# Mixture-of-experts kernel: a taken-branch prefetch hint for each expert's overflow branch on three engines

## The chip, the cores and the metric

The kernel runs on one core of a Trainium2 chip. The metric is the device time of one execution in microseconds (us), the median of several runs. A core has five engines with an instruction stream of their own each: TensorE (PE in the rows; PEld is its weight load), VectorE (DVE), ScalarE (ACT), GpSimd (POOL) and SyncE (SP, which here issues most DMAs). Each engine has a sequencer that reads the stream, waits on semaphores, takes branches and hands work to the engine; a row with a q behind the engine's name (PEldq, DVEq) is the sequencer's.

## The reference

Two transformer blocks on 256 tokens of width 1024. The change lies in the last part, a mixture of experts:

```python
def hierarchical_moe(h, w_group, b_group, w_expert, b_expert, w_gate, w_up, w_down):
    ...
    gates = ...   # top 1 group of 4, then top 2 of its 4 experts, per token
    y = jnp.zeros_like(t)
    for e in range(N_EXPERTS):                     # 16
        a = jax.nn.silu(t @ w_gate[e]) * (t @ w_up[e])
        y = y + gates[:, e:e + 1] * (a @ w_down[e])
    return y.reshape(h.shape)
```

Each expert has 1024 x 512 gate and up weights and 512 x 1024 down weights in float32, 6.3 MB in all. A token goes to two of the 16 experts.

## The kernel before, in words

The kernel does not compute every expert for every token. It numbers the tokens of each expert, gathers the first 64 of them with one-hot products, runs the expert on these 64 slots, and adds the weighted result back with another one-hot product. Tokens beyond the first 64 are handled in up to four further passes of 32, 64, 64 and 32 slots (`MORE`, line 152), which are nested under conditions.

The function `experts` (line 1839) is one unrolled loop over the 16 experts, traced in order. For expert e:

- `ahead` and `take` (lines 1811 and 1831) issue the loads of weight tiles on SP, as far ahead as 20 tiles of 1 MB go; an expert takes six of them.
- `gated` (line 1902) finishes the expert before: VectorE multiplies its down product by the gates (L1912), ScalarE and VectorE split the result into two parts (L1916, L1917).
- `hidden` (line 1863) is the gate and up product: 32 matmuls of 128x512 into the bank `gu`, then the SiLU on ScalarE (L1872) and the product on VectorE (L1873).
- Products for other experts fill TensorE's wait for these two: for even e the combination of the pair before (`combine`, bank `cmb`), for odd e the one-hot transposes (`places`, bank `ohT`), and half of the gather for the next pair (`gather`, bank `ga`).
- `down` (line 1876) transposes the hidden values (bank `aT`, L1887) and does 16 matmuls into the bank `dn`.
- `others` (line 1942) tests the expert's bit in a word that all engines hold in a register, and under it lies the code of the overflow passes, `more` (line 1920):

```python
with tc.If((words[i] & (1 << e)) > 0):        # L1946
    more(e, w, p, S)
    if i + 1 < len(MORE):
        others(e, w, i + 1)
```

Each engine has this branch in its own stream. An engine that has no overflow to do jumps over the body and adds to two semaphores what the body would have added (the EVENT_SEMAPHORE rows of L1946). With this data only expert 0 has overflow, of one pass of 32 slots. Work after the branch on other engines, and the reuse of the expert's weight tiles, waits for these semaphores. Order on an engine is that of the trace, with `issue_after(x)` placing what is traced inside it behind instruction x.

All matmuls are issued in `mm` at L223, so the rows tell them apart by the banks' names.

Of the kernel before, what the change touches and what calls it, by code (L numbers as in the profile page):

```python
# [12 lines left out]
AF = mybir.ActivationFunctionType  # L13
# [5 lines left out]
P = 128  # L19
# [122 lines left out]
def tile_model(ctx: ExitStack, tc: tile.TileContext, aps: dict, out: bass.AP, dbg=None):  # L142
# [38 lines left out]
    def banks(**tags):  # L181
        """a new sharing of the banks: A for the main stream, F for those beside it, others for what names them"""
        pst.close()
        psum["pool"] = pst.enter_context(tc.tile_pool(name="ps" + "".join(tags), bufs=1, space=PSUM))
        psum["tags"] = tags
# [7 lines left out]
    # work beside the main stream, traced in steps between its tiles of weights  # L193
# [3 lines left out]
    def pool(name):  # L197
        """a pool of the stream that is traced: the second one has its own end of the memory"""
        return tc.tile_pool(name=name, bufs=1, side="right" if tagsel[0] == "F" else "left")
# [51 lines left out]
    def wsplit(raw, a, n):  # L251
        """split [P, a, n] in pieces of 1024 columns; returns k -> (hi, lo) of [P, n]"""
# [18 lines left out]
    # ---------------------------------------------------------------- modulation  # L271
# [35 lines left out]
    def gemv(m, s):  # L307
        """2048 columns of the modulation: row 32 * g of the result holds columns 512 * g.. (row 32 * g + 1 for the
        context's condition)"""
# [45 lines left out]
    def mods(m, parts):  # L355
        """the modulation of layer m (of the second block for m = 2)"""
# [16 lines left out]
    # ---------------------------------------------------------------- norms  # L373
# [16 lines left out]
    def rstd_x():  # L390
        """1 / rms of the rows of X, from the sums of squares of their halves"""
        rs = sp.tile([P, 2], F32, tag="rs2", name="rs2", bufs=2)
        nc.gpsimd.tensor_add(rs, SSQ[:, :, 0], SSQ[:, :, 1])  # L393
        rsq(rs, rs, 1.0 / D, EPS)
        return rs

    def norm_steps(a, sh, hi, lo, src=None, xsplit=None):
        """hi/lo [P, KT, 256] get the split of norm(x) * a + sh, transposed"""
# [46 lines left out]
    def out_proj(w, lh, ll, gd, first=None, after=None):  # L445
        """X += g * (lhs^T @ w); lh, ll [P, KT, 256]; first(n): the tile of the first four blocks of rows; after(n):
        what comes once half n of the columns is done"""
# [23 lines left out]
    # ---------------------------------------------------------------- layer 0 mixer  # L471
    def hybrid(begin, gates):
        w = aps["hy_w_in"]
        with ExitStack() as stack:
# [47 lines left out]
            # xBC^T and dt^T, weights stationary: [channel, lat 256 | ctx 256]  # L522
# [38 lines left out]
            # rope tables with the gains of the norms  # L561
# [10 lines left out]
            def rope(x, nh, i, b, dst):  # L572
                """dst = rope(x * gain); x [P, nh, 64]"""
# [9 lines left out]
            # k, v for latents and context  # L583
# [36 lines left out]
            # q  # L620
# [28 lines left out]
            # z^T  # L649
# [34 lines left out]
            # attention: the scores of a head lie in the queue ahead of the transposes of the head before  # L684
# [41 lines left out]
            # group norm of y * silu(z), [channel, tok]  # L726
# [24 lines left out]
            def first(n):  # L751
                # these rows of w_out follow the (kv, d) partition order of the attention output
# [10 lines left out]
    def ssd(hp, xbc, dtT, gy):  # L763
        # dt, decays: [tok, blk(lat0, lat1, ctx0, ctx1), dir*8 + head]
# [13 lines left out]
        # inclusive sums over the chunk, and the sums beyond each token (over both chunks for the context)  # L778
# [20 lines left out]
        # token-major copies of x and b  # L799
# [21 lines left out]
        # chunk states [ (g, n), head-in-group, p ]  # L821
# [23 lines left out]
        # per pair of heads (j, j + 4): decays from rows of inclusive sums, then both directions in one product  # L845
# [49 lines left out]
    def softplus(o, x, pool, name):  # L895
        """o = max(x, 0) + ln(1 + exp(-|x|))"""
# [6 lines left out]
    # ---------------------------------------------------------------- swiglu  # L903
# [65 lines left out]
    # ---------------------------------------------------------------- layer 1 mixer  # L969
# [37 lines left out]
    def final(i):  # L1007
        """x = norm(x) * w"""
# [11 lines left out]
    # ---------------------------------------------------------------- second block  # L1020
    def proj_tok(w, c0, hi, lo):
        """[tok, 512] per block of tokens: (h @ w[:, c0:c0 + 512])"""
# [10 lines left out]
    def proj_T(w, c0, hi, lo):  # L1033
        """(h @ w[:, c0:c0 + 512])^T of 256 tokens: two banks of [channel, 2 tiles, tok]"""
# [12 lines left out]
    def log_forget(f, lf, kf):  # L1047
        """lf = log sigmoid(f), kf = 1 - sigmoid(f); the floor of the forget gate is softmax over the one
        layer less itself, zero for any hg_lb"""
# [10 lines left out]
    def hg_ctx(hi, lo, S):  # L1060
        """final states [d, dir, head, e] of the context"""
        w = aps["w_in_2"]
        with pool("hgc") as hp:
# [4 lines left out]
            for dr in range(2):  # L1068
# [6 lines left out]
                for b in range(2):  # L1075
                    o = bank()
                    # sums beyond each token in the direction of the scan
# [25 lines left out]
    def hg_raw(hi, lo, raw, i):  # L1103
        """the logits of forget gate i (as U), or q for i = 2, all [channel, head, tok]"""
# [9 lines left out]
    def hg_gates(raw, hp, bufs):  # L1114
        """log decays A = log sigmoid(f) and U = -log(1 - sigmoid(f)) (in the place of f) of both directions"""
# [15 lines left out]
    def hg_rest(hi, lo, raw, i):  # L1131
        """values (i = 0) or weighted output gate, [tok, (head, e)]"""
# [9 lines left out]
    def hg_core(A, U, q, v, g, S, mh, ml, res):  # L1142
        """attention between tokens whose indices in the chunk first differ in bit lv, with decays split at the
        boundary between them; lv 7 is that between the chunks. Queries grow by A, keys decay by U: the input gate
        and the decay up to the boundary"""
        with tc.tile_pool(name="hgl", bufs=1) as hp:
# [4 lines left out]
            # the scores across the chunks take the place of U, which is done with by then  # L1151
# [64 lines left out]
    def head_norm(o, g, pre, sq, mh, ml, k0, c):  # L1216
        """rms norm over each head (of o * pre), times g (the weighted gate); the split transposed into mh/ml"""
# [18 lines left out]
    def dn_conv(i, hi, lo, lat, res, dp, hp, bufs):  # L1236
        """projects q, k or v (i = 0, 1, 2); returns the steps that convolve it, to [channel, head, tok]"""
# [39 lines left out]
    def dn_gates(hi, lo, res, dp, hp):  # L1277
        """gate and decay logits, [b_fwd, b_bwd, a_fwd, a_bwd] x head"""
# [11 lines left out]
    def dn_core(res, S, lat, dp, both):  # L1290
        """delta rule over two chunks of 128; S [d, dir, head, e] is left by the context and read by the latents;
        the split of the latents' output goes to the pair res["done"]"""
# [4 lines left out]
        with pool("dn") as hp:  # L1297
# [36 lines left out]
            # per chunk and direction, [s, head, t]: decays between tokens as sums of what lies between them, then  # L1334
            # the inverse of the unit triangular system by doubling its diagonal blocks: with y the inverse of the
            # blocks, y a y joins their early tokens (rows) with their late ones (columns)
# [49 lines left out]
            def half(t, m, i):  # L1386
                """columns of [P, 4, 128] in the first (i = 0) or second halves of blocks of 2 m"""
                return t.rearrange("p h (n s m) -> p h n s m", s=2, m=m)[:, :, :, i, :]
# [78 lines left out]
            if lat:  # L1467
                # 1 / |q| per token; q itself stays as it is, its norm goes on the output
# [96 lines left out]
    def mixer2(Shg, Sdn, a, sh):  # L1565
        w = aps["w_in_2"]
        with tc.tile_pool(name="m2", bufs=1) as mp, ExitStack() as right:
# [6 lines left out]
            with tc.tile_pool(name="hgr", bufs=1) as rp:  # L1574
# [28 lines left out]
                # the projections are done with the input: the mixer's output takes its place  # L1603
# [12 lines left out]
    # ---------------------------------------------------------------- mixture of experts  # L1616
    def router(a, sh):
        """the router's weights and bias with the modulation in them; returns the steps that follow the halves of
        X: its transposition and the logits [tok, block, group and expert]"""
# [32 lines left out]
    def route(lg, rp):  # L1652
        """lg [P, 2, 20]: membership [P, 2, 16] of the top 2 experts in the top group, and the gates as later()"""
# [8 lines left out]
        def first_max(v, n, name):  # L1662
            """per group of 4: the maximum and the one-hot of its first place"""
# [49 lines left out]
    def moe(a, sh, lg, rsx):  # L1713
        """gates and places of the tokens, then the experts: each takes its first 64 tokens, and under branches of
        its own the others"""
        with tc.tile_pool(name="moe", bufs=1) as mp:
# [4 lines left out]
            def onehot(q):  # L1721
                """[tok, block, expert of the pair, slot], and the same times 1 / rms(x)"""
# [12 lines left out]
            def gather(ohr, xg, ks):  # L1735
                """the tokens' x, modulated, [d, slot], for blocks ks of d; the last two as the returned steps"""
# [24 lines left out]
            # the sums over the experts start from x  # L1761
# [7 lines left out]
            with tc.tile_pool(name="rt", bufs=1) as rp:  # L1769
                sel, later = route(lg, rp)  # L1770
                # number of each token among its expert's tokens, from 1; 0 for those of other experts
# [13 lines left out]
                # bit e of word i: expert e has tokens for pass i of MORE  # L1785
# [9 lines left out]
    def wloader(wp):  # L1795
        """loads the experts' weights in the order of their use, as far ahead as the buffers go: those of wp first,
        then the ring's; returns next(), the next tile, and ahead(n), which loads on until n are waiting"""
# [8 lines left out]
        # at last the weight of the final norm  # L1806
# [32 lines left out]
    def experts(out_, start, rsx, pos, gate, over, oh, xg, onehot, newx, gather):  # L1839
        take, ahead = wload  # L1840
        with tc.tile_pool(name="ex", bufs=1) as mp:
# [6 lines left out]
            def rows(g, S=64):  # L1848
                return slice(S * g, S * g + S)

            def places(oh):
                """one-hot of two experts with the slots on the partitions, in either order"""
# [10 lines left out]
            def hidden(x, w, S=64):  # L1863
                """the gated hidden values of S slots, [(part of the columns, slot), column]"""
# [7 lines left out]
                nc.scalar.activation(sl[:, :c], o[:, :c], AF.Silu)  # L1872
                nc.vector.tensor_mul(sl[:, :c], sl[:, :c], o[:, c:2 * c])  # L1873
                return sl, last
# [208 lines left out]
```

## Time and profile before

| what | value |
|---|---|
| median of three runs | 1602.34 us (1599.1 to 1608.84) |
| the profiled execution | known by its span, 1600.3 us from the first to the last instruction |
| mean granted TensorE clock | 0.960 of full speed |
| TensorE busy | 1457.0 us, 91% of the span |
| VectorE, ScalarE busy | 830.2 us and 641.9 us |
| the experts' part | from about 1257 us to the end; experts 1 to 15 take 1294.4 to 1585.7 us |

The span lies 2.0 us under the median of the three runs. The share of TensorE's busy time over the whole span says little of the experts' part, which is the last fifth; there the rows are read junction by junction, a junction being the stretch from the last down matmul of one expert to the first gate and up matmul of the next.

### The profile page before, as it was taken

The page shows a single profiled execution, that of the slowest core. Times are in us where ns is not written, and L with a number is a line of the kernel's source. Part 1 is how long each engine was busy: PE and PEld are TensorE (multiplying, and loading weights), DVE is VectorE, ACT ScalarE, POOL GpSimd, SP SyncE. Part 2 cuts the span into 40 slices and gives each one's busy share as a digit, 9 for nine tenths or more (in the row PEclk, how much of TensorE's full clock was granted, in tenths as well). Part 3 has the DMA queues.
Part 4 walks back from the last instruction along what each step waited for, and adds up shares of the span by engine and source line. Part 5 has one row for each costly group of instructions (what it writes and reads, how often), then busy time and mean ns, then how long its engine had stood idle before and what let it go on. Part 6 is the DMA issues. An engine that isn't in the chain of part 4 may idle for free. (4 is left out here: it accounts for less than half of the span.)

```text
span 1600.3 us, 21546 instructions
## 1 busy us (share of the span) xinstructions
PE 1457.0 (91%) x8503; PEld 1057.3 (66%) x8503; DVE 830.2 (52%) x1405; ACT 641.9 (40%) x1030; POOL 147.4 (9%) x210
## 2 busy tenths in 40 slices
PE   4989999999999999998999979889988977887886
PEld 2666446768776799997788869878877533433342
DVE  1464654644454578655455577799745322222222
ACT  2653344554454335344444445946523111111111
POOL 2012110000002000001000001244121000000000
PEclk9998999999999999999999989999999889899999
DMA  9344688766787743333555543332204948888870
GB/s 363 126 158 172 228 297 267 262 247 226 258 296 282 254 132 110 115 132 106 185 183 183 180 163 106 106 106 80 79 1 163 388 176 319 317 318 311 312 274 29
DMA packets 133418, 320.54 MB, mean 200 GB/s; under 512 B 6576, under 2 KB 25008, under 8 KB 124048
## 3 DMA queue, kind: packets, MB, share of 16 engines
q1 hardware_dynamic: 130848, 311.31, 55.5%
q0 software_dynamic: 2416, 7.15, 1.3%
q8 instruction: 100, 1.64, 0.4%
q14 instruction: 54, 0.44, 0.1%
HBM read 317.36 MB, written 1.07 MB: 199 GB/s over the span
## 5 line engine op out<-in xcount | busy, mean ns | idle before, releaser
L243 DVE TENSOR_TENSOR whl<-raw,whl 128x1024 fp32r<-128x1024 f32 x252 | 312.7, 1244 | 283.1 <-ACT whl L243 282.6
L243 ACT CAST whl<-raw 128x1024 fp32r<-128x1024 f32 x252 | 262.8, 1047 | 336.3 <-PE b L223 124.6
L223 PE MATMUL gu<-whl,f_hi 128*128 128x512 f32 (+1 forms) x768 | 229.0, 381 | 0.0
L223 PEld LDWEIGHTS gu<-whl,f_hi 128*128 128x128 f32 x768 | 138.8, 188 | 36.5 <-issue 5.1
L223 PE MATMUL gu<-whl,f_lo 128*128 128x512 f32 (+1 forms) x384 | 144.5, 378 | 0.0
L223 PE MATMUL gu<-mw,xg 128*64 128x512 f32 x384 | 100.8, 681 | 32.5 <-PEq L1946 23.9
L223 PE MATMUL do<-whl,th 128*128 128x512 f32 x352 | 114.3, 401 | 0.0
L223 PEld LDWEIGHTS gu<-mw,xg 128*64 128x64 f32 x384 | 35.2, 156 | 95.4 <-issue 92.1
L223 PE MATMUL gv<-raw,csil 128*32 128x512 f32 x576 | 80.9, 629 | 19.0 <-DMA raw<-in_ada_w_dram 19.0
L223 PEld LDWEIGHTS gu<-whl,f_lo 128*128 128x128 f32 x384 | 72.3, 188 | 15.6 <-issue 1.9
L223 PE MATMUL b<-l_hi,whl 128*128 128x256 f32 x384 | 75.4, 296 | 4.0 <-DVE whl L243 4.0
L223 PEld LDWEIGHTS do<-whl,th 128*128 128x128 f32 x352 | 65.4, 188 | 20.2 <-issue 5.9
L223 PE MATMUL b<-s_hi,whl 128*128 128x256 f32 x384 | 73.0, 286 | 0.0
L223 PE MATMUL do<-whl,tl 128*128 128x512 f32 x176 | 69.1, 396 | 0.0
L1912 DVE SCALAR_TENSOR_TENSOR yf<-dn,gs,gbc 64x512 f32<-64x512 f32 (+1 forms) x36 | 25.9, 720 | 78.7 <-PEq L1946 74.6
L223 PEld LDWEIGHTS b<-l_hi,whl 128*128 128x128 f32 x384 | 62.0, 196 | 6.8 <-DVE whl L243 4.2
L223 PEld LDWEIGHTS b<-s_hi,whl 128*128 128x128 f32 x384 | 60.4, 189 | 0.0
L1873 DVE TENSOR_TENSOR sl<-sl,gu 128x256 f32<-128x256 f32 (+1 forms) x17 | 7.0, 413 | 98.0 <-ACT sl L1872 98.0
L1264 DVE SCALAR_TENSOR_TENSOR qkv<-raw,cols_sb,qkv 128x189 f32<-128x189 f32 (+3 forms) x112 | 56.6, 554 | 0.0
L223 PE MATMUL b<-whl,l_hi 128*128 128x512 f32 x160 | 52.8, 410 | 4.0 <-DVE whl L243 2.6
L223 PE MATMUL b<-l_lo,whl 128*128 128x256 f32 x192 | 55.6, 290 | 0.0
L223 PE MATMUL b<-s_lo,whl 128*128 128x256 f32 x192 | 54.6, 285 | 0.0
(547 smaller groups left out, 2661.7 us busy)
## 6 DMA issues: line engine op xcount, KB each, us to landing
raw<-in_ada_w_dram SPq DMA_DIRECT2D x48, 1024.0 KB, 5.0
raw<-in_w_in_dram SPq DMA_DIRECT2D x28, 1024.0 KB, 5.0
raw<-in_w_mod_dram SPq DMA_DIRECT2D x24, 1024.0 KB, 5.0
mw<-in_w_gate_dram SPq DMA_DIRECT2D x48, 512.0 KB, 10.7
mw<-in_w_up_dram SPq DMA_DIRECT2D x48, 512.0 KB, 11.0
raw<-in_ffn_w_gate_dram SPq DMA_DIRECT2D x22, 1024.0 KB, 5.1
raw<-in_ffn_w_up_dram SPq DMA_DIRECT2D x22, 1024.0 KB, 5.2
mw<-in_w_down_dram SPq DMA_DIRECT2D x22, 1024.0 KB, 10.0
```

The lines of the kernel that those rows point to most:

```text
L223: return nc.tensor.matmul(o, l, r, start=start, stop=stop)
L243: return nc.scalar.copy(hi, src), nc.vector.tensor_sub(lo, src, f32(hi))
L1264: nc.vector.scalar_tensor_tensor(yy, ov[:, r0 + dr:r1 + dr, c0 + dc:c1 + dc], c[:, 3 * a + b:3 * a + b + 1], yy, op0=ALU.mult, op1=ALU.add)
L1873: nc.vector.tensor_mul(sl[:, :c], sl[:, :c], o[:, c:2 * c])
L1912: nc.vector.scalar_tensor_tensor(yv, o[v, :c], gs[v, :], g2[v, n * c:(n + 1) * c], op0=ALU.mult, op1=ALU.mult)
```

## The change

`hidden` returns its last matmul, its SiLU and its product as well, and the branch has a name. Behind the last gate and up matmul on TensorE, behind the SiLU on ScalarE and behind the product on VectorE stands one hint each, which tells that engine's sequencer that the branch `over{e}_0` is likely taken (the jump over the body is the taken side). The nested branches have names and no hints; GpSimd and SyncE have none. The rest of the diff takes out comments and docstrings.

```diff
             def hidden(x, w, S=64):
...
-                nc.scalar.activation(sl[:, :c], o[:, :c], AF.Silu)
-                nc.vector.tensor_mul(sl[:, :c], sl[:, :c], o[:, c:2 * c])
-                return sl, last
+                s1 = nc.scalar.activation(sl[:, :c], o[:, :c], AF.Silu)
+                s2 = nc.vector.tensor_mul(sl[:, :c], sl[:, :c], o[:, c:2 * c])
+                return sl, last, (last, s1, s2)
...
-                with tc.If((words[i] & (1 << e)) > 0):
+                with tc.If((words[i] & (1 << e)) > 0, label=f"over{e}_{i}"):
                     more(e, w, p, S)
...
-                sl, last = hidden(xg[:, :, rows(h)], w)
-                # the products that fill the waits for the hidden values and their transposes
+                sl, last, marks = hidden(xg[:, :, rows(h)], w)
+                for m, en in zip(marks, (nc.tensor, nc.scalar, nc.vector)):
+                    with tc.issue_after(m.ins):
+                        tc.mark_branch_hint_location(f"over{e}_0", hint="LikelyTaken", engines=[en.engine])
+
                 fill = None
                 with tc.issue_after(last.ins):
```

## Rows read from the trace of the kernel before

**Rows 1.** The page: the span, and the group of L1912 (busy, mean, idle, releaser).

```profile
span 1600.3 us, 21546 instructions
...
L1912 DVE SCALAR_TENSOR_TENSOR yf<-dn,gs,gbc 64x512 f32<-64x512 f32 (+1 forms) x36 | 25.9, 720 | 78.7 <-PEq L1946 74.6
```

**Rows 2.** Waits of PE, 1294 to 1586 us: total us, times, longest.

```profile
PE gu L223 <- PEq L1946: 37.2, 13, 4.5
PE gu L223 <- DVE y L1917: 6.0, 1, 6.0
...
PE gu L223 <- ACTq L1946: 2.0, 1, 2.0
```

**Rows 3.** Instructions of L1946, whole span: ns min/median/max, first and last start.

```profile
L1946 DVEq COMPARE_BRANCH  x18: 47/56/67, 1269.1 to 1580.8; - x18
L1946 ACTq COMPARE_BRANCH  x18: 38/45/50, 1269.9 to 1581.5; - x18
L1946 PEldq COMPARE_BRANCH  x18: 91/6188/7445, 1270.5 to 1582.0; - x18
```

**Rows 4.** Timeline of the junction behind expert 2: start, us, what [idle before].

```profile
1332.54 1.89 PE L223 MATMUL dn<-mwr,aT 128*64 128x512 f32 x8
...
1337.45 1.53 DVE L1912 SCALAR_TENSOR_TENSOR yf<-dn,gs,gbc 64x512 f32<-64x512 f32 x2 [5.21 <-PEq L1946]
...
1337.77 5.35 PE L223 MATMUL gu<-mwr,xg 128*64 128x512 f32 x16 [3.34 <-PEq L1946]
```

**Rows 5.** L1946 in 1325 to 1340 us: the same junction.

```profile
L1946 PEldq COMPARE_BRANCH  x1: 6228/6228/6228, 1330.9 to 1330.9; - x1
```

**Rows 6.** L1946 in 1345 to 1360 us: the junction behind expert 3.

```profile
L1946 PEldq COMPARE_BRANCH  x1: 6233/6233/6233, 1350.6 to 1350.6; - x1
```

**Rows 7.** L1946 in 1374 to 1379 us: the junction behind expert 4.

```profile
L1946 PEldq COMPARE_BRANCH  x1: 3413/3413/3413, 1374.8 to 1374.8; - x1
```

**Rows 8.** Timeline of the junction behind expert 4.

```profile
1379.01 7.09 PE L223 MATMUL gu<-mw,xg 128*64 128x512 f32 x32 [0.64 <-PEq L1946]
```

**Rows 9.** DMA queues, 1294.4 to 1585.7 us: packets, MB, share of 16 engines.

```profile
q1 hardware_dynamic: 34416, 80.22, 74.7%
q8 instruction: 41, 0.67, 1.0%
```

**Rows 10.** DMA queues, 1334.4 to 1335.8 us.

```profile
q8 instruction: 1, 0.02, 5.0%
```

**Rows 11.** A window inside a burst (last columns: clock, DMA share, GB/s); slices of 1374 to 1379 us.

```profile
1321.00:1335.00 14.00, 13.16 (x74) 6.48 (x70) 2.00 (x7) 1.67 (x4) 0.00 (x0) 0.99 1.04 399
...
GB/s 360 426 344 344 164 131 98 66 66 33 16 33 16 33 147 33 0 0 0 0 0 0 0 66 0 0 0 0 0 0 0 0 0 0 0 0 0 0 0 131
```

**Rows 12.** The 32 gu matmuls behind experts 2 to 14, columns as above.

```profile
1337.77:1346.56 8.79, 8.79 (x32) 3.12 (x32) 0.00 (x0) 0.00 (x0) 0.81 0.90 307
1360.14:1369.90 9.76, 9.76 (x32) 3.87 (x31) 0.00 (x0) 0.00 (x0) 0.72 1.03 400
1379.01:1386.10 7.09, 7.08 (x32) 2.61 (x32) 0.00 (x0) 0.00 (x0) 1.00 0.78 289
...
sum 109.32, PE 109.29 PEld 38.82 DVE 0.00 ACT 0.00; mean PE 8.41 PEld 2.99 DVE 0.00 ACT 0.00
```

**Rows 13.** Weight loads behind expert 3 (timeline of PEld).

```profile
1357.37 0.13 PEld L223 LDWEIGHTS gu<-mw,xg 128*64 128x64 f32 x1 [4.13 <-issue]
1360.14 0.29 PEld L223 LDWEIGHTS gu<-mw,xg 128*64 128x64 f32 x3 [2.64 <-issue]
```

**Rows 14.** Timeline of PE: gu behind experts 0 and 1.

```profile
1295.28 9.77 PE L223 MATMUL gu<-mw,xg 128*64 128x512 f32 x32 [3.35 <-PEq L1946]
...
1317.18 5.35 PE L223 MATMUL gu<-mw,xg 128*64 128x512 f32 x16 [2.00 <-ACTq L1946]
```

**Rows 15.** A window of two experts: PE, PEld, DVE, ACT, POOL busy (instructions), clock, DMA.

```profile
1378.40:1416.60 38.20, 31.04 (x166) 14.57 (x166) 9.92 (x22) 6.39 (x13) 0.00 (x0) 0.96 0.90 332
```

**Rows 16.** Waits of SP's queue, 1294 to 1586 us.

```profile
SPq L1824 <- PEq L1946: 166.8, 13, 21.5
```

## Prediction

> **What bounds the kernel now.** I read the page first, and in it the group of L1912: VectorE sits idle 74.6 us before this one line, and what it waits for is not TensorE's work but TensorE's sequencer at L1946, the overflow branch [rows 1]. The list of TensorE's own waits says the same from the other side: 37.2 us in 13 junctions between experts end with that sequencer, 6.0 us in one with a VectorE step, 2.0 us in one with ScalarE's sequencer [rows 2]. Then the instructions of L1946: the branch takes VectorE and ScalarE about 0.05 us, TensorE 6.2 us in the median and 0.09 us at the least [rows 3]. The 0.09 us is expert 0, the one that goes into the body; the long ones jump over it. So the jump is the taken side, and on TensorE alone it is dear.
>
> The timeline of the junction behind expert 2 shows what it costs: the last down matmul ends at 1334.43, the branch, begun at 1330.9, ends at 1337.13 [rows 5], and only then come VectorE's next step (1337.45) and the next matmul (1337.77), after 3.34 us of nothing [rows 4]. The matmul queue covers the first 3.5 us of the branch and no more. In the listing of DMA queues one packet of an instruction queue, 0.02 MB, lies at 1334.4 to 1335.8 us, inside that branch [rows 10]: the sequencer has jumped to code that it does not have and waits for its fetch.
>
> The price has two levels. Behind expert 4 the branch took 3.41 us [rows 7], and there the weight traffic had just run dry (360 to 426 GB/s falling to nothing within the first microsecond or two of that window), while around expert 2's branch it ran at 399 GB/s [rows 11]. So a fetch is about 3.4 us beside quiet queues and 6.2 us beside busy ones. At the junction behind expert 4 the matmuls hid it: TensorE stood 0.64 us [rows 8].
>
> [...]
>
> **The change part by part.** The junction behind expert 4 serves as the model of one whose branch is ready in time: 0.64 us and 7.09 us at full clock.
>
> TensorE's hint, experts 1 to 15. Of the 13 junctions that the sequencer ended, one is behind expert 0 (3.35 us) [rows 14]; its wait is for the nested branch, which gets no hint, so nothing goes there. The other 12 hold 37.2 - 3.35 = 33.85 us; at 0.64 us each they would hold 7.7 us: 26.2 us go. Behind expert 3 the pause is 6.02 us; here one weight load ran at 1357.37 and the next only at 1360.14 [rows 13], so after the jump the sequencer stood a second time: the target lay near the end of a fetched piece, and the next piece was missing too. Without both it gives 6.02 - 0.64 = 5.4 us. Behind expert 1 the pause of 2.0 us ends with ScalarE [rows 14], which had its gather to finish: nothing goes.
>
> The clock. The 13 stretches of gate and up matmuls behind experts 2 to 14 add to 109.32 us [rows 12]; at 7.09 us they are 92.2 us: 17.1 us go. Behind experts 0 and 1 they stay as they are.
>
> Sum: 26.2 + 5.4 + 17.1 = 48.7 us if every hinted fetch is ready and no second fetch stands. The second one is not hinted, though, and other junctions can come to lie as expert 3's does, once one hint per expert shifts the code behind it. I keep one such junction and let it win only what the others win on average, (48.7 - 8.1) / 12 = 3.4 us in place of 8.1 (5.4 + 2.7 of clock): 44.0 us remain. The profile is of an execution of 1600.3 us, 2.0 us under the median of the runs, which I keep as what lies around: 1602.3 - 44.0 = 1558 us.
>
> Is the lead enough? The hint stands behind the last gate and up matmul. Those of expert 4 ended at 1369.90 [rows 12] and its branch began at 1374.8 [rows 7], 4.9 us later; for odd experts it is 4.1 us (1346.56 to 1350.6) [rows 6, 12]. The sequencer may pass the hint earlier than the matmul ends, not later. A fetch of 6.2 us is then at most 2.1 us late at the branch, and the 16 down matmuls of 3.65 us, queued by then, cover that. From both sides: a hint that comes only at the matmul's end costs nothing visible, one that is passed at the matmuls' start has about 7 us more.
>
> The hints themselves. No row shows one. The nearest are the sequencer's own branch, 0.05 us on VectorE and ScalarE and 0.09 us on TensorE when it falls through [rows 3]; 15 of them on TensorE would be 1.4 us if nothing hid them. TensorE's lie behind matmuls already queued, so I take nothing. VectorE's and ScalarE's lie where those engines wait for TensorE next, and win nothing, as their branches have no fetch to wait for. From the dear side a hint could bring one fetch too many and cost 3.4 to 6.2 us where it displaces code needed at once; expert 0's hint is the sure case of a wrong one, since its branch is not taken: nothing to 6.2 us, I take nothing, by the cheap fall-through row.
>
> What is late next? The weights. SP's issues wait for TensorE's branch in all 13 loads of later tiles (166.8 us) [rows 16], so they move forward with it. In 291.3 us 80.2 MB are loaded [rows 9]; inside a burst the rate is 399 GB/s [rows 11], so they need 201 us, and 291.3 - 48.7 = 242.6 us stay. Fetches beside traffic that now hardly pauses will all be of the 6.2 us kind, which the lead above allows for. Behind the branch VectorE's L1912 starts some 3 us earlier, and is not waited for until the next combination.
>
> [...]
>
> **The rivals.** First, the hint does nothing: the branch's taken side is another than I read, or a fetch starts at the branch alone. Against: the cheap branch is the one into the body [rows 3]. Time: 1602 us.
>
> Second, the hinted piece is lost where TensorE passes into a new piece between hint and branch. The instruction queue made 41 fetches for 15 experts [rows 9]. With 15 targets and, I assume, 15 pieces behind the targets (one fetch follows each jump), 11 are passages inside an expert. Two experts run 166 matmuls [rows 15], so 83 each, and 50 to 52 of them lie between hint and branch (16 down, 16 gather, 10 for transposes and gates, and 8 or 10 for combination or places): 0.61 of the 11 passages, about 7 of 15 junctions. There the branch stalls as now. Gain 48.7 x 8/15 = 26 us, time 1576 us.
>
> [...]
>
> **How the numbers follow.** All fetches in time: 0.66, 1558 us, with its own range 1549 (all 48.7 us and the clock behind expert 1 too, less the scatter of runs) to 1568 (a wrong hint's 6.2 us and one more second fetch). Half of them lost: 0.16, 1576 us. Nothing: 0.10, 1602 us. Slower: 0.06, 1619 us; 0.02 for the rest. The range runs from 1547 to 1587 us and holds the first two. One per cent, 16 us, is about what a measurement of this kernel tells from no change; 1586 us is the bound. Faster by more: 0.82, the first two cases and nothing else; within it 0.12; slower 0.06.
>
> **What would show it.** Right: TensorE's branch at L1946 under 3.4 us, down to some 0.1 us; 0.6 to 0.9 us of pause in most junctions; the 32 matmuls at 7.09 us and clock 1.00; DMA gaps between bursts nearly gone; as many long instruction fetches as before, only earlier. [...]

## The result, and the profile after

The changed kernel took 1557.24 us (median of four runs, 1548.81 to 1566.19) beside 1603.12 us for the kernel before (four runs, 1599.1 to 1608.84): a ratio of 0.973, with a 95% interval of 0.967 to 0.978. That is 45.9 us less. The forecast was 1558 us.

The profiled execution of the changed kernel is the slowest of its four. Its page begins with a longer time than the median, and has these two rows among others (the instruction queue: packets, MB, share; the group of L1912: busy, mean, idle, releaser):

```profile
span 1564.2 us, 21594 instructions
...
q8 instruction: 89, 1.46, 0.4%
...
L1912 DVE SCALAR_TENSOR_TENSOR yf<-dn,gs,gbc 64x512 f32<-64x512 f32 (+1 forms) x36 | 25.9, 720 | 52.0 <-PEq L1946 45.6
```

VectorE waits 45.6 us for TensorE's sequencer here, 74.6 us before [rows 1]. The waits of TensorE between experts, 1305 to 1550 us (total us, times, longest), answer to [rows 2]:

```profile
PE gu L223 <- PEq L1946: 12.3, 14, 3.1
...
PE gu L223 <- ACTq L1946: 2.0, 1, 2.0
```

Before, 13 such waits took 37.2 us; now 14 take 12.3 us. The wait of 6.0 us for a VectorE step, the junction behind expert 3, is no longer among them. The instructions of L1946 over the whole span show why (ns, least, median, most):

```profile
L1946 DVEq COMPARE_BRANCH  x18: 53/61/80, 1285.5 to 1543.3; - x18
L1946 ACTq COMPARE_BRANCH  x18: 38/49/66, 1286.2 to 1544.0; - x18
L1946 PEldq COMPARE_BRANCH  x18: 90/350/5854, 1286.9 to 1544.5; - x18
```

TensorE's median branch went from 6188 ns [rows 3] to 350 ns, while VectorE's and ScalarE's stayed at 0.05 to 0.06 us. The hints stand under the line of the build. They cost 31 to 61 ns each:

```profile
L2073 PEldq BRANCH_PREFETCH_HINT  x16: 31/31/45, 1280.3 to 1536.6; - x16
L2073 ACTq BRANCH_PREFETCH_HINT  x16: 31/31/50, 1282.9 to 1541.1; - x16
L2073 DVEq BRANCH_PREFETCH_HINT  x16: 39/39/61, 1284.6 to 1541.5; - x16
```

But the largest branch is still 5.85 us. Going through the branches one by one finds three long ones, behind experts 8, 9 and 10, and 0.35 us from there on (L1946 in four short stretches):

```profile
L1946 PEldq COMPARE_BRANCH  x1: 5854/5854/5854, 1433.2 to 1433.2; - x1
...
L1946 PEldq COMPARE_BRANCH  x1: 4982/4982/4982, 1450.8 to 1450.8; - x1
...
L1946 PEldq COMPARE_BRANCH  x1: 1958/1958/1958, 1468.4 to 1468.4; - x1
...
L1946 PEldq COMPARE_BRANCH  x1: 352/352/352, 1483.6 to 1483.6; - x1
```

The timeline of TensorE shows a junction that came out as wished, behind expert 2, and the worst one, behind expert 8 (start, us, what, idle before):

```profile
1343.06 3.65 PE L223 MATMUL gu<-mwr,xg 128*64 128x512 f32 x16 [0.57 <-PEq L1946]
...
1432.92 3.65 PE L223 MATMUL dn<-mw,aT 128*64 128x512 f32 x16
1439.65 5.37 PE L223 MATMUL gu<-mwl,xg 128*64 128x512 f32 x24 [3.08 <-PEq L1946]
```

The pause behind expert 2 was 3.34 us [rows 4] and is 0.57 us. Behind expert 8 a branch of 5.85 us is covered by the down matmuls for all but 3.08 us. The 32 gate and up matmuls by window, behind experts 0, 1, 2, 8 and 9 (the first column is the length, the third from the end the granted clock):

```profile
1305.99:1313.08 7.09, 7.08 (x32) 2.61 (x32) 0.00 (x0) 0.00 (x0) 1.00 0.97 312
1325.24:1334.02 8.78, 8.78 (x32) 2.61 (x32) 0.00 (x0) 0.00 (x0) 0.81 1.03 391
1343.06:1350.15 7.09, 7.08 (x32) 2.61 (x32) 0.00 (x0) 0.00 (x0) 1.00 0.88 328
...
1439.65:1446.74 7.09, 7.09 (x32) 2.63 (x32) 0.00 (x0) 0.00 (x0) 1.00 1.00 367
1456.39:1463.48 7.09, 7.09 (x32) 2.60 (x32) 0.00 (x0) 0.00 (x0) 1.00 1.01 360
```

All stand at 7.09 us and full clock but the one behind expert 1, whose pause is ScalarE's. Before, those behind experts 2 to 14 added to 109.32 us [rows 12]; now they take 92.1 us.

**Where the time went.** The experts' part as a whole, from the first gate and up matmul of expert 1 to the last down matmul of expert 15, is read from one window of each kernel (length, busy of PE, PEld, DVE, ACT, POOL, then clock, DMA share and GB/s). The kernel before:

```profile
1295.30:1585.50 290.20, 242.06 (x1230) 110.73 (x1230) 70.84 (x154) 47.20 (x96) 0.00 (x0) 0.92 0.76 279
```

The changed kernel:

```profile
1306.00:1549.50 243.50, 223.69 (x1230) 105.71 (x1230) 70.99 (x154) 47.22 (x96) 0.00 (x0) 0.99 0.89 332
```

The same 1230 matmuls take 18.4 us less at a clock of 0.99 in place of 0.92, and TensorE idles 19.8 us in place of 48.1: together 46.7 us, all inside experts 1 to 15. Expert 0 adds 4.8 us (38.0 to 33.2 us). That makes 51.5 us, more than the 36.1 us between the two spans. The other 15.5 us were lost ahead of the experts: their first matmul starts at 1272.8 us here and at 1257.3 us in the profile of before. One stretch of that loss, in the routing ahead of the experts; changed kernel:

```profile
1180.00:1210.00 30.00, 27.19 (x138) 20.60 (x138) 9.42 (x17) 8.05 (x14) 9.36 (x8) 0.66 0.00 1
```

Kernel before:

```profile
1180.00:1210.00 30.00, 25.87 (x188) 21.64 (x188) 16.19 (x31) 5.95 (x10) 9.26 (x8) 1.00 0.01 1
```

The code there is the same in both, though the two windows do not cover quite the same instructions, as the changed kernel's execution is already some 7 us behind. The granted clock happened to be 0.66 in one execution and 1.00 in the other. Over the profiles of this study the experts' first matmul starts anywhere from 1257 to 1275 us, with and without hints. So for single changes inside the experts the window of experts 1 to 15 is the finer measure, and I give it beside most times below. It has a scatter of its own: two kernels below whose hints win nothing take 284.3 and 284.0 us in it, 6 us less than the kernel before, most of it at expert 3; the changed kernel takes 243.5 us and, profiled again, 243.0 us. The gain inside it is therefore some 40 to 47 us, and a difference of 6 us from the one profile of before shows nothing by itself.

### The profile page after: what moved, and what is told of

Same layout as the page of the kernel before. It is cut to its first block, busy times and chain, and to the rows that moved or that the text cites. A ratio compares the mean times of both kernels' runs of the same rounds, so it can differ in the third digit from the quotient of the medians.

```text
span 1564.2 us, 21594 instructions
## 1 busy us (share of the span) xinstructions
PE 1452.1 (93%) x8503; PEld 1063.3 (68%) x8503; DVE 830.0 (53%) x1405; ACT 642.1 (41%) x1030; POOL 145.7 (9%) x210
## 3 DMA queue, kind: packets, MB, share of 16 engines
q8 instruction: 89, 1.46, 0.4%
## 5 line engine op out<-in xcount | busy, mean ns | idle before, releaser
L223 PE MATMUL gu<-mw,xg 128*64 128x512 f32 x384 | 88.1, 609 | 9.6 <-PEq L1946 7.5
L223 PEld LDWEIGHTS gu<-mw,xg 128*64 128x64 f32 x384 | 31.7, 140 | 63.3 <-issue 58.9
L1912 DVE SCALAR_TENSOR_TENSOR yf<-dn,gs,gbc 64x512 f32<-64x512 f32 (+1 forms) x36 | 25.9, 720 | 52.0 <-PEq L1946 45.6
L223 PE MATMUL dy<-Y,Q 128*128 128x64 f32 x384 | 48.3, 279 | 1.0 <-DVE Y L1418 0.6
```

The source lines that it names most:

```text
L223: return nc.tensor.matmul(o, l, r, start=start, stop=stop)
L1912: nc.vector.scalar_tensor_tensor(yv, o[v, :c], gs[v, :], g2[v, n * c:(n + 1) * c], op0=ALU.mult, op1=ALU.mult)
```

## The experiments

The question was what the hints do, on which engine, when they come too late, and why three of the fifteen branches stayed long. In each diff a line with + is in the experiment's kernel and a line with - in the kernel it starts from.

**Which engine: TensorE's hint alone.** From the changed kernel:

```diff
-                for m, en in zip(marks, (nc.tensor, nc.scalar, nc.vector)):
+                for m, en in zip(marks[:1], (nc.tensor,)):
```

> Hints on TensorE alone, those of ScalarE and VectorE left out. My theory: the whole gain is TensorE's, so the time is that of the changed kernel, about 1557 us, and TensorE's branches look the same: about 0.35 us each, with three long ones, behind experts 8, 9 and 10. Rival: the other two engines' branches take part; then it is over 1565 us and VectorE's or ScalarE's steps behind the branch come later than in the changed kernel.

Measured: 1556.95 us (1551.67 to 1558.08), a ratio of 0.968 (0.963 to 0.972) to the kernel before; experts 1 to 15 take 240.7 us. Its branch rows and waits read as the changed kernel's:

```profile
L1946 PEldq COMPARE_BRANCH  x18: 90/350/6190, 1277.3 to 1536.8; - x18
```

The same three branches are long (6.19, 4.92 and 1.72 us). TensorE's hint alone brings the whole gain.

**ScalarE's and VectorE's hints alone.**

```diff
-                for m, en in zip(marks, (nc.tensor, nc.scalar, nc.vector)):
+                for m, en in zip(marks[1:], (nc.scalar, nc.vector)):
```

> Hints on ScalarE and VectorE alone. My theory: TensorE's branch stays at a median of 6.2 us and the time at that of the kernel before, 1603 us give or take 6. Rival: these hints win a part; then under 1590 us.

Measured: 1606.08 us over ten runs, ratio 1.000 (0.997 to 1.003); experts 1 to 15 take 284.3 us.

```profile
L1946 PEldq COMPARE_BRANCH  x18: 91/6195/6599, 1279.5 to 1581.8; - x18
```

TensorE's branches are those of before. The two other hints neither win nor cost anything that can be measured in the whole time. One thing differs from before, the junction behind expert 3:

```profile
1360.67 7.09 PE L223 MATMUL gu<-mw,xg 128*64 128x512 f32 x32 [3.24 <-PEq L1946]
```

The pause there is 3.24 us in place of 6.02, though the branch takes 6.19 us and TensorE has no hint. So the second stall that the prediction read there went with the changed program, not with a piece fetched ahead.

**Expert 0's hint, whose branch is not taken.**

```diff
-                for m, en in zip(marks, (nc.tensor, nc.scalar, nc.vector)):
+                for m, en in zip(marks if e else (), (nc.tensor, nc.scalar, nc.vector)):
```

> All hints but those of expert 0, whose branch is not taken. My theory, from the changed kernel's trace: the piece fetched by expert 0's hint is the one to which its nested branch jumps, so without it that branch takes about 3.9 us again instead of 0.37, the pause behind expert 0 is about 3.3 us instead of 0.8, and the matmuls behind it may run 2.7 us longer at a lower clock; everything behind is as in the changed kernel. Rival: expert 0's hint is a wrong one and costs; then expert 0 gets shorter without it.

One execution: 1557.95 us. TensorE takes three branches at expert 0; the middle one is the nested one, which jumps over the remaining passes, and it is the longest. Without expert 0's hint (L1946 in that stretch):

```profile
L1946 PEldq COMPARE_BRANCH  x3: 91/193/3354, 1273.4 to 1295.4; - x3
```

In the changed kernel:

```profile
L1946 PEldq COMPARE_BRANCH  x3: 90/190/372, 1286.9 to 1305.5; - x3
```

So the hint that names the wrong way is the one that made the nested branch short. The pause behind expert 0 is 2.72 us without it and 0.81 us with it, and the gate and up matmuls of expert 1 take 8.78 and 7.09 us: 3.6 us together. The whole time can't show that. The reading that fits is that both branches jump to nearly the same place, so what was fetched for the first serves the second; that is argued from the program, not tested by itself.

**The hint late.** TensorE's hint moves behind the first down matmul; the other two stay.

```diff
-                for m, en in zip(marks, (nc.tensor, nc.scalar, nc.vector)):
+                for m, en in zip(marks[1:], (nc.scalar, nc.vector)):
...
+                        m = mm(o[rows(g, S), :c], ...)
+                        if hint is not None:
+                            with tc.issue_after(m.ins):
+                                tc.mark_branch_hint_location(hint, hint="LikelyTaken", engines=[nc.tensor.engine])
+                            hint = None
```

> TensorE's hint moved behind the first down matmul of its expert, some 0.2 us ahead of the branch; the other hints stay. My theory: what counts is the time between hint and end of the down matmuls; a fetch beside weight traffic needs about 6 us and 3.7 are left, so TensorE's branch takes 5 to 6 us, the pause is 2 to 3.3 us and the time lies between 1585 and 1603 us. Rival: it is not the earlier fetch but something that comes with any hint (where the target is laid); then the time stays at 1557 us and the branch at 0.35 us.

Measured: 1600.73 us over ten runs, ratio 0.998 (0.995 to 1.002); experts 1 to 15 take 284.0 us. The branches, the waits of 1299 to 1586 us, and one hint, behind expert 4, whose branch begins at 1374.1 us:

```profile
L1950 PEldq COMPARE_BRANCH  x18: 90/5976/6403, 1275.6 to 1580.9; - x18
...
PE gu L223 <- PEq L1950: 40.4, 14, 3.5
...
L2077 PEldq BRANCH_PREFETCH_HINT  x1: 36/36/36, 1373.7 to 1373.7; - x1
```

A hint 0.44 us ahead of the branch wins nothing. So it is the early fetch that pays, and not anything else that a hint brings into the program.

**The hint early.** It goes behind the first gate and up matmul.

```diff
-                return sl, last, (last, s1, s2)
+                return sl, last, (first, s1, s2)
```

> TensorE's hint moved ahead, behind the first gate and up matmul. In the changed kernel three branches stay long (behind experts 8, 9, 10: 5.9, 5.0, 2.0 us). My theory: there a piece of code ends between hint and branch, and the target is fetched only once TensorE's sequencer is in the piece that holds the branch; then an earlier hint changes nothing and the same three stay long by about as much. Rival: the lead was too short; then they fall to 0.35 us.

One execution: 1553.7 us; experts 1 to 15 take 241.9 us. The hint leads the branch by 11 to 12 us, and the largest branch is no shorter:

```profile
L1948 PEldq COMPARE_BRANCH  x18: 90/350/5629, 1272.9 to 1533.6; - x18
```

The three long branches are the same ones: 5.63, 5.04 and 2.02 us. Two or three microseconds more of lead buy nothing. The lead is not what they lack.

**Where in the code the branch lies.** In the changed kernel the fetch of the hinted code can be seen in the listing of DMA queues. Behind the hint of expert 8, at 1423.6 us, there is only weight traffic for 12.8 us, and the packet of the instruction queue comes after the branch has begun (1433.2 us); the windows 1423.6 to 1436.4 and 1436.4 to 1438 us:

```profile
q1 hardware_dynamic: 2108, 5.06, 103.9%
...
q1 hardware_dynamic: 279, 0.59, 98.4%
q8 instruction: 1, 0.02, 4.4%
```

By the packets' starts the hinted fetch comes 12.9, 10.9, 8.9 and 5.5 us behind the hints of experts 8, 9, 10 and 11, and 4.0 us in most others. The busy share of the weight queue is no higher there than elsewhere: 103.9% in the window above, 104.6% and 104.8% between hint and packet of experts 4 (1360.9 to 1364.8 us) and 12 (1490.4 to 1494.4 us). What does run through these experts in steps is the place of the code. A packet of this queue is 16 KB (1.46 MB in 89). In the part of the trace that has no branches, from the packet at 36 us to the one at 1224 us, 54 packets go with 13,813 recorded instructions of TensorE (counted up to the next packet, at 1254.7 us), 255.8 a packet: by my estimate from these two counts a piece is 256 instructions. The places that follow are my estimate too, counted in the compiled program in pieces of that size; no trace shows them (one constant, the place of the first instruction, is set so that expert 3's second stall of [rows 13] comes out). By it the hint stands 71 instructions behind the target of the branch before, and the branch 174 or 179. A piece ends this far ahead of the branch:

| expert | instructions from the piece's end to the branch (estimate) | branch, us (measured) |
|---|---|---|
| 8 | 4 | 5.85 |
| 9 | 28 | 4.98 |
| 10 | 47 | 1.96 |
| 11 | 71 | 0.35 |
| 12 | 90 | 0.35 |

In experts 4 to 7 and in 2, 3, 13, 14 and 15 no piece ends between hint and branch by this count, and the branches take 0.35 to 0.37 us. So the theory: the hinted piece is fetched only once the sequencer is in the piece that holds the branch. Experts 9 and 10 carry it: their packets start 2.4 us behind the start of the branch and 0.5 us ahead of it. Expert 8's, 3.4 us behind, comes as a fetch without a hint does (3.7 us behind the branch of expert 2 in the kernel before), so there a late hint cannot be told from a lost one. Two kernels test it, with matmuls put into the second overflow pass, which no expert runs with this data; they change nothing but the place of the code behind them.

The first, by the same count, puts the piece's end 90 to 106 instructions ahead of the branch in experts 2 to 11, and ahead of the hint in experts 12 to 14:

```diff
+                if p == MORE[1][0]:
+                    pad = bank("gu", "U")
+                    for _ in range(59):
+                        mm(pad[:, :P], ident, ident)
```

> The changed kernel with 59 matmuls more in the body of each expert's second overflow pass, which is not run with this data; they only shift the code, so that in every expert the code piece ends at or within some 15 instructions behind the hint. My theory (a piece that ends late between hint and branch is what makes the three long branches): all branches behind experts 1 to 15 take about 0.35 us, all pauses but that behind expert 1 are 0.6 us, and experts 1 to 15 take about 4 us less than in the changed kernel (243.6 us there), 1553 us. Rival: position does not matter; then there are long branches again.

Measured: 1551.24 us (1546.71 to 1558.35), ratio 0.970 (0.965 to 0.975); experts 1 to 15 take 239.7 us. Branches, and waits of 1292 to 1533 us:

```profile
L1950 PEldq COMPARE_BRANCH  x18: 90/347/462, 1271.7 to 1526.9; - x18
...
PE gu L223 <- PEq L1950: 7.2, 12, 0.9
```

No branch is long any more.

The second puts the end a few instructions ahead of the branch in experts 2 to 13, 5 to 14 by the count put on record:

```diff
+                    for _ in range(59 if e % 2 else 58 if e else 39):
```

> The same with other numbers of matmuls (39, 59 or 58) in bodies that are not run: by my count the code piece ends 5 to 14 instructions ahead of the branch in experts 2 to 13, as it does in expert 8 of the changed kernel. My theory: the branches behind experts 2 to 13 take 5 to 6 us although every hint stands, pauses are 2 to 3.1 us, and the time is 1580 to 1600 us. Rival: position does not matter; then 1557 us and few long branches.

Measured: 1594.18 us over ten runs, ratio 0.993 (0.991 to 0.996); experts 1 to 15 take 281.1 us. Branches and the waits of 1307 to 1590 us:

```profile
L1950 PEldq COMPARE_BRANCH  x18: 90/6062/6372, 1288.8 to 1585.5; - x18
...
PE gu L223 <- PEq L1950: 37.9, 14, 3.4
```

All hints stand where they stood, 8.5 to 9.4 us ahead of the branches, and yet the branches behind experts 2 to 12 take 5.8 to 6.4 us (behind expert 13 4.03 us, where it was 3.78 us before) and TensorE waits as before. Code that never runs took away most of the gain, and in the other kernel it removed the last long branches. Both kernels came out as the theory said beforehand.

**What the pause does to the clock.** The other half of the gain was to come from the clock. To fill the pause without a hint, the kernel before gets products of no use behind the last down matmul of experts 1 to 15, first six:

```diff
+                if e:
+                    with tc.issue_after(lastdn[0].ins):
+                        busy = bank("gu", "U")
+                        for _ in range(6):
+                            mm(busy, ident, w[5][:, 1, :512])
```

> The kernel before, without hints, with six matmuls more (128x512, results unused) behind the down matmuls of experts 1 to 15, ahead of the branch: 2.7 us of work at full clock in a pause of 3.3 us. It tells the two parts of the gain apart. My theory: the branch and the fetch stay, the pause is filled and so the clock stays at its upper level; the 32 matmuls behind take 7.09 us instead of 8.5 to 8.8, and the time falls by about 15 to 17 us, to 1586 us. Rival: the lower clock has another cause than the pause; then 1603 us or more and the 32 matmuls stay at 8.5 us or above.

Measured: 1639.28 us, ratio 1.023 (1.017 to 1.029); experts 1 to 15 take 314.7 us. I had mis-sized the products, at half of what they take; one junction:

```profile
1384.89 5.42 PE L223 MATMUL gu<-mw,cst 128*128 128x512 f32 x12
1390.87 7.09 PE L223 MATMUL gu<-mw,xg 128*64 128x512 f32 x32 [0.56 <-PEq L1946]
```

Six of them take 5.4 us, more than the pause, so the time rose; the clock came back all the same. The second try has `range(3)`:

> The kernel before with three matmuls more ahead of the branch in place of six: in the run before each took 0.90 us, not 0.45 as I had reckoned, so that six overfilled the pause by 2 us an expert. Three are 2.7 us. My theory: pauses of about 0.6 to 0.9 us, the 32 matmuls at 7.09 us, and a time some 15 us under that of the kernel before, about 1587 us: the clock's part of the gain alone. Rival: the extra work costs what it wins elsewhere; then 1600 us or more.

Measured: 1601.44 us over ten runs, ratio 0.999 (0.995 to 1.003). The same junction, the waits of 1296 to 1581 us, and two windows of gate and up matmuls:

```profile
1377.78 2.84 PE L223 MATMUL gu<-mw,cst 128*128 128x512 f32 x6
1381.18 7.09 PE L223 MATMUL gu<-mw,xg 128*64 128x512 f32 x32 [0.56 <-PEq L1946]
...
PE gu L223 <- PEq L1946: 9.7, 13, 2.7
...
1381.18:1388.27 7.09, 7.09 (x32) 2.62 (x32) 0.00 (x0) 0.00 (x0) 1.00 0.95 312
1399.17:1406.26 7.09, 7.09 (x32) 2.63 (x32) 0.00 (x0) 0.00 (x0) 1.00 0.85 277
```

The branches are as long as before (6.2 us), but the gate and up matmuls run at 7.09 us behind experts 3 to 14, where the fill left 0.7 us of pause or less; nine of these twelve ran slower before. (They do so behind expert 1 too, where ScalarE's pause of 2.0 us stayed.) All fifteen take 111.0 us in place of 127.9. So the lower clock of before does come from TensorE standing idle: with the idle time filled and nothing else changed it goes. The time that I expected did not come: experts 1 to 15 take 283.8 us, 6.4 us less than before, not some 15 us less. The products fill 2.8 us of a pause of 3.3, but cost their length where no pause was (behind experts 4, 13 and 14, 0.6 to 0.9 us before). Behind expert 2 TensorE stood another 2.97 us, which the view puts down to a VectorE step, as it does behind expert 3 in the kernel before; in both the matmuls start 3.0 to 3.3 us after the branch has ended and 2.3 us after one more packet of the instruction queue has started, so I read it as a second fetch. Of the 16.9 us of clock, 10.5 went back so. The 6.4 us that are left are within the interval of the whole time, and the kernels whose hints win nothing take 284.3 and 284.0 us without any filling: this run shows the clock come back, but no gain in time.

**Changed kernel and padded kernel side by side**, to see whether the last three branches matter in the whole time:

> The changed kernel once more, beside the next one on the same chip. My theory: three long branches as before, experts 1 to 15 in about 243 us, 1557 us.

> The kernel with shifted code once more, to compare with the changed kernel directly. My theory: no long branch behind experts 1 to 15, about 239.7 us for them, 4 us under the changed kernel. Rival: the difference of 6 us between the two so far is scatter of the clock in earlier stages; then the two are equal in time, and only the branches differ.

Measured: 1557.87 us for the changed kernel, ratio 0.971 (0.965 to 0.976), and 1559.34 us for the padded one, 0.971 (0.966 to 0.976), in six runs each. In the traces experts 1 to 15 take 243.0 and 239.8 us, so the padding wins 3 to 4 us there both times; in the whole time it does not show under a scatter of some 15 us, and I don't claim it as a faster kernel.

## Why the prediction was right, step by step

**The bound.** Right. TensorE's sequencer at the taken branch set the end of each junction; with TensorE's hint alone the gain is all there (1556.95 us).

**The pauses: 26.2 us in twelve junctions and 5.4 us behind expert 3.** The mechanism right, the sum a little high. Behind experts 2 to 14 the pauses went from 39.84 to 11.49 us, 28.4 us in place of 31.6. The missing 3.2 us are experts 8 and 9, which still pause 3.08 and 2.08 us instead of 0.64, less what the others gain by pausing 0.57 us. I had set aside 4.7 us for one more second fetch like expert 3's; none came. Expert 3's own pause went altogether (6.02 to 0.57 us), but some 2.7 us of that are not the early fetch's: the pause is 3.24 us in the kernel without TensorE's hint and 3.33 us in the one with the late hint. No kernel with hints, on whichever engine, has a second stall; how the changed program ended it was not tested.

**The clock: 17.1 us.** Right: 109.32 to 92.1 us, 17.2 us. The size scatters, though: the two kernels whose hints win nothing take 107.3 and 105.6 us there. That a pause costs clock was shown by filling it: all fifteen stretches took 111.0 us in place of 127.9. But as I had read the profile of before, a long pause goes with a slow start (clock 0.81 behind the 3.34 us of expert 2, 0.72 behind the 6.02 us of expert 3, 1.00 behind the 0.64 us of expert 4 [rows 2, 4, 8, 12]), and that is too simple (see the last section).

**Behind expert 0: nothing.** Wrong. I gave the nested branch no gain and expert 0's hint a cost of nothing to 6.2 us. The pause fell from 3.35 to 0.81 us and the gate and up matmuls from 9.77 [rows 14] to 7.09 us, 5.2 us together, and it is the "wrong" hint that does it. This error and the 4.7 us that I had held back lie on the same side: the terms as measured add to 28.4 + 17.2 + 5.2 = 50.8 us, and the forecast had 44.0. That the whole time came within 2 us of it is partly luck, as the terms were sized on one profile, the longest of its kind. From the first gate and up matmul of expert 0 to the last down matmul of expert 15 it takes 328.2 us, while the kernels without TensorE's hint and with the late one take 319.7 and 322.1 us; with TensorE's hint in time it is 276.2 to 276.8 us (the changed kernel twice, and TensorE's hint alone). By these profiles the gain is 43 to 52 us.

**Behind expert 1: nothing.** Right: 2.03 us of pause, still ScalarE's, and 8.78 us.

**The lead: 4.1 to 4.9 us.** Mis-sized, on the safe side. The sequencer passes the hint while the matmuls ahead of it are still queued (expert 8's hint is passed at 1423.6 us, and the matmuls ahead of it end at 1428.1 us; in all 16 experts the hint is passed 2.5 to 4.5 us before that end), so the lead is 7.9 to 9.6 us behind experts 2 to 15. The late hint, with 0.44 us of lead at expert 4 and branches of 5.98 us in the median, shows that the lead matters at all.

**The hints' own price: nothing.** Right: 31 to 61 ns each, and no gain or loss from those of VectorE and ScalarE.

**What is late next.** The loads of later tiles moved forward as argued: SP's issues now wait 94.2 us for TensorE's branch in place of 166.8 [rows 16], and the rate over experts 1 to 15 rose from 279 to 332 GB/s. No gate and up matmul waits for a weight; TensorE itself, 223.7 of 243.5 us busy, is the bound now. One sign failed: I expected as many instruction fetches as before. The program makes 89 in place of 100. In experts 1 to 15 it makes 30, two for each branch, in place of 41 [rows 9]; which ones fell away was not followed up.

**The rivals.** The first (nothing) is out. The second, the hinted piece lost where TensorE passes into a new piece between hint and branch, is real, and I had its size wrong in two ways. It strikes three branches, not seven: by the count five experts (8 to 12) have such a passage, and behind experts 11 and 12, where it lies 71 and 90 instructions ahead of the branch, the branch took 0.35 us. The three cost 3 to 4 us in all, not the 23 of that case, since the down matmuls cover two of them in part and one wholly (pauses of 3.08, 2.08 and 0.57 us), and little clock was lost: none in this profile, 1.4 us behind expert 8 in the second one of the changed kernel (8.53 us at 0.83). The padded kernel with the ends just ahead of the branches is this rival at full strength: it keeps 8.1 us of the gain. What in the chip makes the fetch late there was not shown. The trace shows the starts of the packets: 3.4 us behind the start of the branch in expert 8, 3.0 us ahead of it in expert 11, and in most experts 4.0 us after the hint, ahead of the branch. The slower outcome, 1619 us, would take an extra fetch of some 6.2 us at each of seven passages, and no run shows one: outside the junctions TensorE idles 6.3 us in the window of experts 1 to 15 in either kernel, and the fetches there became fewer, 30 in place of 41.

## What to carry to other kernels

Where an engine's sequencer ends a wait, look at the duration of its branches before looking at the work: here a jump with the fetch of its code inside it [rows 10] took 6.2 us beside weight traffic, and a hint 7.9 to 9.6 us ahead made that 0.35 us in most experts. Only the engine whose sequencer was the bound needed the hint: 1556.95 us with TensorE's alone, 1606.08 us with only the other two. Then check every branch by itself. Three of the fifteen hinted ones still took 5.85, 4.98 and 1.96 us, by the count those where a new piece of code begins 4 to 47 instructions ahead of the branch; and code that never runs, put in ahead, made all of them short (0.46 us at the most) or most of them long (6.06 us in the median).

## What the runs showed that was not expected

Code that is never run changes the time: between two kernels that differ in such code alone, experts 1 to 15 take 239.7 and 281.1 us.

A hint for a branch that is not taken paid, through a nested branch that, by the program, jumps to nearly the same place (3.92 us before, 0.37 us after).

The lower clock does not follow from the length of a pause alone. In the changed kernel pauses of 3.08 and 2.08 us (behind experts 8 and 9) were followed by matmuls at 1.00, and one of 2.03 us behind expert 1 by matmuls at 0.81. With TensorE's hint alone the same pause behind expert 1, 2.01 us, was followed by 7.09 us at full clock. In the padded kernel with the long branches the matmuls behind experts 3, 7 and 11 kept 7.09 us after pauses of 2.8 to 3.4 us, while the eight other long ones behind experts 2 to 12 lost; with the late hint the same three, 3, 7 and 11, kept it. Where filling left 0.7 us or less of pause, the granted clock was 1.00 every time, in twelve junctions of one kernel and thirteen of the other. What decides where the pause isn't filled stays open.

Even a branch of 0.35 to 0.37 us leaves a pause between the last down matmul and the next gate and up matmul: 0.57 us behind nine experts of the changed kernel, 0.63 us behind expert 6.
